# Splitting the second mixer's input projections, and opening the second MLP's accumulators with transposes

## The chip, the core and the metric

The kernel is one program on one core of a Trainium2 chip. Its metric is the device time of one execution in microseconds; the time given for it is the median of three runs. Five engines matter here and run side by side, each through its own instructions in order: TensorE (PE in the profile, with its weight loads as PEld), VectorE (DVE), ScalarE (ACT), GpSimd (POOL), and SyncE (SP), which here only issues the transfers from HBM. All of them wait for one another through semaphores.

## The reference

The input is 256 tokens of 1024 fp32 features. Two layers, each a mixer and an MLP with a residual add behind each, and a norm at the end:

```python
for layer in range(DEPTH):              # 2
    h = rmsnorm(x, mix_norm[layer])
    y = mixer_ab(h, ...) if layer % 2 == 0 else mixer_c(h, ...)
    x = x + y
    x = x + sq_relu_mlp(rmsnorm(x, mlp_norm[layer]), w_up[layer], w_down[layer])
return rmsnorm(x, final_norm)

def mixer_c(h, w_in, conv_w, conv_b, w_r, b_r, w_i, b_i, lam, w_out):
    gate, xr = jnp.split(h @ w_in, 2, axis=-1)               # w_in: 1024 x 2048
    xr = causal_depthwise_conv(xr, conv_w) + conv_b          # width 4
    y = rg_lru(xr, w_r, b_r, w_i, b_i, lam) * jax.nn.gelu(gate)
    return y @ w_out                                         # 1024 x 1024
```

`rg_lru` multiplies xr by two block-diagonal matrices (8 blocks of 128 x 128 each), takes sigmoids, and runs a linear recurrence over the tokens. `sq_relu_mlp` is `square(relu(h @ w_up)) @ w_down` with 4096 hidden features. The weights of the second mixer's input, 8 MB, the two MLPs', 64 MB, and the rest are all read once from HBM.

## The kernel before

**Layout.** x is kept transposed as eight tiles xT[0] to xT[7], each 128 features by 256 tokens. A projection's output chunk (128 features) is the sum of eight products over k; each holds a 128 x 128 block of weights in TensorE and streams the 256 columns of tile k. The two MLPs, their down projections and most of their inputs are split: an fp32 value is a rounded high part and a rest (`split_act` for activations; `weights` for weights, by a rounding copy and a subtraction), both of type fp32r, and a product is the sum of three fp32r products, high with high, high with rest, rest with high. The first mixer, the second mixer's input projections, its gates and its output projection multiply plain fp32 instead, which the profile shows as two records for each product.

**Weights.** A unit is the weights of one output chunk (or of one row chunk in the down and output projections), 512 KB; two units make a piece. `piece` gives each piece its home when the program is built. There are five raw buffers (raw0 to raw4, one piece each) and eight pairs of buffers (wh0/wl0 to wh7/wl7). A piece of MLP weights lands in a raw buffer, and each of its units is split into a pair: `weights` issues, for each half of a unit, a rounding copy (`move`, on VectorE or ScalarE, whichever the planner picks) and a subtraction (VectorE). A piece that is used as plain fp32 is not split: the first five of a sequence of such pieces stay in raw buffers, and each later one lands with its two units in the wh and the wl buffer of one pair. Raw buffers and pairs are each handed out in turn. So before the change the second mixer's xr weights and its gate matrices (`ri`) sit in raw buffers, its gate-branch and output weights in pairs.

**Order.** The whole program is recorded as operations with their dependences, and a planner (`Plan.schedule`) sorts each engine's instructions by list scheduling with costs and latencies written in the file; ten rounds, the shortest forecast is emitted. On TensorE an operation goes when it is ready, by priority, and priorities fall along the written order. The splits' priority is lowered a little (`LIFTS`). Transfers keep the written order among themselves on SP's one queue: a transfer that waits for its buffer holds all those written behind it.

**The second mixer.** At the end of the first MLP `out_cols` finishes the accumulators two chunks at a time, and `residual_chunk` adds them to xT, scales by the norm's gain and squares for the norm. Then come, in written order: xr chunks 0 and 1, the norm's sum (`finish_norm`: a product with ones, a square root, a reciprocal giving rstd), xr chunks 2 to 7 with the gates of finished chunks between them, the gate-branch chunks, and the output projection (`out_rows` for rows 0 to 3, then `out_cols` for 4 to 7). Each xr chunk has a tail on VectorE (times rstd, then the four taps of the conv); the gates' sigmoids, exponentials and roots run on ScalarE, which loads another table whenever the kind of function changes. Projections and gates take the four PSUM banks b in turn; a bank is taken again when its last reader is done.

**The second MLP.** Its down projection is not transposed: five accumulators in PSUM hold tokens by features, so that the output can be written as it is. x has to be added there. Before the change this happens on TensorE: in 16 of the row steps, d = 4 to 19, one of the 8 chunks of one of the two token halves is added by two fp32r products of 128 columns with an identity (`identr`), one for the high part and one for the rest of xT[k].

Of the kernel before, what the change touches and what calls it, by code (L numbers as in the profile page):

```python
# [7 lines left out]
F32R = mybir.dt.float32r  # L8
# [3 lines left out]
P = 128  # L12
S = 256
D = 1024
KD = D // P
# [4 lines left out]
NRAW = 5  # L20
# [306 lines left out]
def hybrid_trunk(ctx, tc, x, mix_norm, mlp_norm, w_up, w_down, ab_w_in, ab_conv_w, ab_ln_g, ab_ln_b,  # L327
# [8 lines left out]
    def tl(name, shape=(P, S), dt=F32):  # L336
        return sb.tile(list(shape), dt, name=name)
# [48 lines left out]
    def copy(out, a):  # L386
        return plan.add("V", [("tensor_copy", (out, a), {})], [out], [a], {"V": vcost(fsize(out), not is_psum(a))})
# [27 lines left out]
    def mms(items, after=()):  # L415

        calls, outs, ins, c = [], [], [], 0.0
        for o, l, r, st, sp in items:
            calls.append(("matmul", (o,), {"lhsT": l, "rhs": r, "start": st, "stop": sp, "skip_group_check": True}))
            outs.append(o)  # L420
            ins += [l, r]
            c += max(fsize(r) / 2400.0, 0.0533) * (1 if l.dtype == F32R else 4) + (0.0135 if l.dtype == F32R else 0.005)
        return plan.add("T", calls, outs[:1], ins, {"T": c}, after=after)

    def transposes(items):
        calls = [("transpose", (o, i, d), {}) for o, i, d in items]
        return plan.add("T", calls, [items[0][0]], [i for _, i, _ in items] + [items[0][2]],
                        {"T": 0.109 * len(items)})

    def dma(out, in_, size):  # L430
        return plan.add("S", [("dma_start", (out, in_), {})], [out], [in_], {"S": 0.0}, size=size)


    ident = tl("ident", (P, P))
    identr = tl("identr", (P, P), F32R)
    ones = tl("ones", (P, P))
    pcol = tl("pcol", (P, P))
    wcol = tl("wcol", (P, P))
# [60 lines left out]

    pieces, units = [], []
    homes, pairs = [], {}
    turn = {"raw": 0, "pair": 0, "whole": 0}

    def piece(kind, ap, whole=True):
        n = len(pieces)
        pieces.append((kind, ap))
        us = [len(units), len(units) + 1]  # L510
        units.extend([(n, 0), (n, 1)])
        turn["whole"] = turn["whole"] + 1 if whole else 0
        if turn["whole"] > NRAW:
            i = turn["pair"] % NSPL
            turn["pair"] += 1
            homes.append((whs[i], wls[i]))
        else:
            raw = raws[turn["raw"] % NRAW]
            turn["raw"] += 1
            homes.append((raw[:, :1024], raw[:, 1024:]))  # L520
        if not whole:
            for u in us:
                pairs[u] = turn["pair"] % NSPL
                turn["pair"] += 1
        return us

    def cols(w, c, whole=True):

        return piece("c", w.rearrange("(k p) c -> p k c", p=P)[:, :, c * P:(c + 2) * P], whole)

    def rows(ap, whole=True):
        return piece("r", ap, whole)

    taken = [0, 0]
    got = {}
# [51 lines left out]
    for us in (((u_gate, 4), (u_val, 0)), ((u_q, 8), (u_k, 12))):  # L587
        for c in (0, 2):
            for u, at in us:
                u += cols(w_in, at + c)  # L590
    u_v = rows(wv[:, 0:4]) + rows(wv[:, 4:8])
    wo = ab_w_out[0].rearrange("(k p) c -> p k c", p=P)
    u_o = {}
    for k in (4, 6, 0, 2):
        u_o[k], u_o[k + 1] = rows(wo[:, k:k + 2])
    LAG, TAIL = 4, 4

    def mlp_units(layer):
        up, dn = [], []
        wd = w_down[layer].rearrange("(f p) c -> p f c", p=P)  # L600
        for f in range(0, NF + LAG, 2):
            if f < NF:
                up += cols(w_up[layer], f, False)
            if f >= LAG:
                dn += rows(wd[:, f - LAG:f - LAG + 2], False)
        return up, dn

    u_up, u_dn, u_xr, u_gt, u_co = {}, {}, [], [], []
    u_up[0], u_dn[0] = mlp_units(0)
    for c in range(0, 8, 2):  # L610
        u_xr += cols(c_w_in[0], 8 + c)
        if c == 2:
            u_r, u_i = piece("ri", None)
    for c in range(0, 8, 2):
        u_gt += cols(c_w_in[0], c)
    wco = c_w_out[0].rearrange("(k p) c -> p k c", p=P)
    for k in range(0, 8, 2):
        u_co += rows(wco[:, k:k + 2])
    u_up[1], u_dn[1] = mlp_units(1)


# [9 lines left out]
    xsrc = x[0].rearrange("(t p) d -> p t d", p=P)  # L631
    R = lambda ap: ap.rearrange("a (b p) -> (a b) p", p=P)
    make_identity(nc, ident)
    copy(identr, ident)
    memset(ones, 1.0, "V")
    memset(eps_t, EPS, "V")
    act(tiny[:, 60:61], eps_t, AF.Sqrt)
# [29 lines left out]
    def par(name, c):  # L667
        i = col0[name] + c
        return pcol[:, i:i + 1]


    def project(dst, u, xs):
        w = weights(u)
        for k in range(KD):
            mms([(dst, w[k], xs[k], k == 0, k == KD - 1)])

    def project_wide(b, u, xs):

# [4 lines left out]
    def split_act(src, scale, tag, bufs, engs="V"):  # L683
        t = rot(tag, bufs, (P, 2 * S), F32R)
        h, lo = t[:, :S], t[:, S:]
        if scale is None:
            move(h, src)
            tt(lo, src, h.bitcast(F32), OP.subtract, engs)
        else:
            move(h, src, scale)  # L690
            stt(lo, src, scale, h.bitcast(F32), OP.mult, OP.subtract)
        return h, lo, t

    def scaled(src, scale):
        t = rot("xg", KD)
        move(t, src, scale)
        return t

    def residual_chunk(k, acc, gname, g0, xs):
        tt(xT[k], acc, xT[k], OP.add)  # L700
        g = par(gname, g0 + k)
        xs[k] = scaled(xT[k], g) if gname == "mix" else split_act(xT[k], g, "x", KD)
        if k in (0, KD - 2):
            act(ssum if k == 0 else sumb, xT[k], AF.Square)
        else:
            sq = rot("nsq", 2)
            act(sq, xT[k], AF.Square)
            if k < KD - 2:
                tt(ssum, ssum, sq, OP.add)
            else:  # L710
                tt(sumb, sumb, sq, OP.add)
# [219 lines left out]
        t = [bank("a") for _ in range(4)]  # L931
        return [t[c // 2][:, (c % 2) * S:(c % 2 + 1) * S] for c in range(KD)]

    def out_mm(acc, c, w, xp, start, stop):
        if not isinstance(w, tuple):
            return mms([(acc, w[c], xp, start, stop)])
        mms([(acc, a[:, c, :], b, start and n == 0, stop and n == 2)
             for n, (a, b) in enumerate(((w[0], xp[0]), (w[0], xp[1]), (w[1], xp[0])))])

    def out_rows(accs, u, xp, first):  # L940
        w = weights(u)
        for c in range(KD):
            out_mm(accs[c], c, w, xp, first and c % 2 == 0, False)

    def out_cols(accs, us, xps, done):
        ws = [weights(u) for u in us]
        for c0 in range(0, KD, 2):
            for c in (c0, c0 + 1):
                for i, (w, xp) in enumerate(zip(ws, xps)):
                    out_mm(accs[c], c, w, xp, False, i == len(us) - 1)  # L950
            done(c0)
            done(c0 + 1)

# [187 lines left out]

    blocks = []

    def down_mm(block, w, hp, first, last):
        t, c0, c1, b = block
        s = slice(t * P, (t + 1) * P)
        wh, wl = (q.rearrange("p a b -> p (a b)")[:, c0:c1] for q in w)
        mms([(b[:, :c1 - c0], p[:, s], q, first and n == 0, last and n == 2)
             for n, (p, q) in enumerate(((hp[0], wh), (hp[1], wh), (hp[0], wl)))])

    xsp = {}

    def down_rows(u, hp, d):
        w = weights(u)
        if d == 0:
            blocks.extend((t, c0, c1, bank("a")) for t, c0, c1 in ((0, 0, 512), (0, 512, D), (1, 0, 512), (1, 512, 768)))
            blocks.append((1, 768, D, banks["b"].pop(bank_at["b"] % 4)))
        for block in blocks:
            down_mm(block, w, hp, d == 0, False)
        if 4 <= d < 20:  # L1160

            k, t = divmod(d - 4, 2)
            if t == 0:
                xsp[k] = split_act(xT[k], None, "r", 2)
            for bt, c0, c1, b in blocks:
                if bt == t and c0 <= k * P < c1:
                    mms([(b[:, k * P - c0:(k + 1) * P - c0], q[:, t * P:(t + 1) * P], identr, False, False)
                         for q in xsp[k][:2]])

    _, us, hs = mlp(1, xs, down_rows)  # L1170
    ws = [weights(u) for u in us]
# [2 lines left out]
    for n, block in enumerate(blocks):  # L1174
        t, c0, c1, b = block
        xg, fc = xg2[t], fcol[:, t]
        for i in range(len(us)):
            down_mm(block, ws[i], hs[i], False, i == len(us) - 1)

        part = fc[:, n % 2 if n < 2 else n - 2:][:, :1]  # L1180
        act(fsq[:, :c1 - c0], b[:, :c1 - c0], AF.Square, accum=part)
        tt(xg[:, c0:c1], b[:, :c1 - c0], gfin[:, c0:c1], OP.mult)
        if c1 < D:
            ts(fc[:, 4:5], part, 1.0 / D, EPS if c0 == 0 else fc[:, 4:5], OP.mult, OP.add)
            continue
        act(fc[:, 5:6], part, AF.Sqrt, scale=1.0 / D, bias=fc[:, 4:5])
        recip(fc[:, 6:7], fc[:, 5:6])
        for h in (slice(0, 512), slice(512, D)):
            move(xg[:, h], xg[:, h], fc[:, 6:7])
            dma(o_dst[:, t, h], xg[:, h], P * 2048)  # L1190
# [32 lines left out]
```

## Time and profile before

| | |
|---|---|
| time, median of 3 runs (lowest to highest) | 589.08 us (588.99 to 589.18) |
| profiled execution: its time, and the span of its instructions | 588.62 us, 586.8 us |
| TensorE busy, mean granted clock | 579.9 us (99%), 0.999 |
| VectorE busy | 413.1 us (70%) |
| ScalarE busy | 289.7 us (49%) |
| read from HBM | 97.11 MB |
| second mixer: input projections and gates | from 307.6 to 370.2 us |
| second mixer: output projection | from 370.2 to 397.9 us |

Busy time is the time in which at least one instruction of the engine runs. TensorE's products overlap one another: the pace of a stream is the time from the start of one to the start of the next, and not the duration of one, which is longer. The same holds for two instructions that follow each other on VectorE or ScalarE. Nearly all instructions are recorded under line 310, the planner's emission, so that groups are told apart by their tiles: x is the scaled and split input of an MLP, xg the scaled plain input of a mixer, f the split hidden activations, raw, wh and wl the weights, r the split xT that the identity products read, arena everything that is small or short-lived. The 1.8 us by which the profiled execution's time exceeds its span lie around the instructions.

### The profile page before, as it was taken

To read this page: it belongs to the slowest core of one execution; us is meant where nothing else is said; L and a number is where in the kernel's file an instruction comes from. 1 tells how busy PE (TensorE), PEld (TensorE's weight loads), DVE (VectorE), ACT (ScalarE), POOL (GpSimd) and SP (SyncE) were. 2 spreads that over 40 slices of the span, in tenths; PEclk is the share of its full clock that TensorE was granted. 3 is DMA by queue.
4 is the path that set the end of the run, shared out by engine and by line. 5 is a ranking of instruction groups with operands and counts; after the bars stand their busy time and mean duration, and the time that the engine had idled before them with its cause. 6 is when DMAs were issued, how large, how long until landed. Compare 5 with 4: busy or idle time off the path is not lost.

```text
span 586.8 us, 9026 instructions
## 1 busy us (share of the span) xinstructions
PE 579.9 (99%) x3305; PEld 510.2 (87%) x3305; DVE 413.1 (70%) x946; ACT 289.7 (49%) x592; POOL 2.8 (0%) x22
## 2 busy tenths in 40 slices
PE   9999999999999999999999999999999999999995
PEld 8888768889999999999998888888888888888885
DVE  2599998599777767677446777559876767767732
ACT  4131435467554555555321798327555555545523
POOL 1000000000000000000000000000000000000000
PEclk9999999999999999999999999999999999999999
DMA  7997704125664665566677005924645664563001
GB/s 222 324 382 256 258 1 144 71 70 163 203 212 145 191 217 166 166 205 203 218 223 280 1 0 157 370 83 143 196 164 180 196 198 144 185 212 107 1 1 72
DMA packets 67612, 98.74 MB, mean 168 GB/s; under 512 B 3212, under 2 KB 55664, under 8 KB 67568
## 3 DMA queue, kind: packets, MB, share of 16 engines
q1 hardware_dynamic: 67568, 98.17, 50.7%
q8 instruction: 26, 0.43, 0.3%
q14 instruction: 18, 0.15, 0.1%
HBM read 97.11 MB, written 1.05 MB: 167 GB/s over the span
## 4 chain that ended last, share of the span: by engine, by line
PE 99%; ACT 0%; DVE 0%; issue 0%; ACTq 0%
PE bank_b L310 56%; PE bank_a L310 42%; ACT arena L395 0%; DVE arena L310 0%; ACT arena L310 0%; DVE ones L310 0%; DVE tiny L310 0%; DVE eps L310 0%; ACTq L310 0%
## 5 line engine op out<-in xcount | busy, mean ns | idle before, releaser
L310 DVE TENSOR_TENSOR wl<-raw,wh 128x512 fp32r<-128x512 f32 x256 | 175.1, 690 | 84.5 <-ACT wh L395 76.3
L395 ACT ACTIVATE wh<-raw 128x512 fp32r<-128x512 f32 x223 | 139.5, 630 | 168.2 <-PE bank_b L310 104.3
L310 PE MATMUL bank_b<-x,wh 128*128 128x512 f32 x512 | 184.7, 401 | 0.0
L310 PE MATMUL bank_b<-x,wl 128*128 128x256 f32 x512 | 143.8, 281 | 0.0
L310 PEld LDWEIGHTS bank_b<-x,wh 128*128 128x128 f32 x512 | 96.4, 188 | 20.9
L310 PEld LDWEIGHTS bank_b<-x,wl 128*128 128x128 f32 x512 | 96.8, 189 | 0.1
L310 PE MATMUL bank_a<-f,wh 128*128 128x256 f32 x512 | 93.2, 283 | 0.0
L310 PEld LDWEIGHTS bank_a<-f,wh 128*128 128x128 f32 x512 | 79.6, 191 | 1.4
L310 PE MATMUL bank_a<-f,wl 128*128 128x256 f32 x256 | 72.4, 283 | 0.0
L310 PE MATMUL bank_a<-wh,f 128*128 128x512 f32 (+1 forms) x256 | 72.2, 364 | 0.0
L310 PE MATMUL bank_b<-xg,raw 128*128 128x256 f32 x288 | 64.1, 379 | 0.0
L310 PEld LDWEIGHTS bank_b<-xg,raw 128*128 128x128 f32 x288 | 54.1, 190 | 7.3
L310 PEld LDWEIGHTS bank_a<-wh,f 128*128 128x128 f32 x256 | 45.9, 188 | 9.1
L310 DVE SCALAR_TENSOR_TENSOR arena<-arena,wcol 128x256 f32<-128x256 f32 x120 | 49.5, 478 | 0.0
L310 PEld LDWEIGHTS bank_a<-f,wl 128*128 128x128 f32 x256 | 49.0, 192 | 0.0
L310 PE MATMUL bank_a<-wl,f 128*128 128x512 f32 (+1 forms) x128 | 46.5, 363 | 0.0
L310 PE MATMUL bank_a<-arena,wh 128*128 128x256 f32 x128 | 34.4, 381 | 0.0
L310 PE MATMUL bank_a<-arena,wl 128*128 128x256 f32 x128 | 33.9, 379 | 0.0
L310 DVE TENSOR_TENSOR relu<-bank_b,relu 128x256 f32<-128x256 f32 x64 | 26.7, 417 | 10.1 <-ACT relu L310 10.1
L310 ACT ACT_TABLE_LOAD x24 | 30.8, 1283 | 3.0 <-PE bank_b L310 1.9
L310 ACT ACTIVATE relu<-relu 128x256 f32<-128x256 f32 x64 | 26.1, 411 | 8.2 <-DVE relu L310 5.1
L310 ACT ACTIVATE relu<-bank_b 128x256 f32<-128x256 f32 x64 | 23.6, 369 | 11.6 <-PE bank_b L310 11.6
(125 smaller groups left out, 594.3 us busy)
## 6 DMA issues: line engine op xcount, KB each, us to landing
raw<-in_w_up_dram SPq DMA_DIRECT2D x64, 512.0 KB, 5.7
raw<-in_w_down_dram SPq DMA_DIRECT2D x64, 512.0 KB, 4.8
raw<-in_c_w_in_dram SPq DMA_DIRECT2D x8, 512.0 KB, 5.4
raw<-in_ab_w_in_dram SPq DMA_DIRECT2D x6, 512.0 KB, 7.8
wh<-in_ab_w_in_dram SPq DMA_DIRECT2D x5, 512.0 KB, 8.7
wl<-in_ab_w_in_dram SPq DMA_DIRECT2D x5, 512.0 KB, 8.8
raw<-in_ab_w_in_dram SPq DMA_DIRECT2D x8, 256.0 KB, 5.7
wh<-in_ab_w_out_dram SPq DMA_DIRECT2D x4, 512.0 KB, 10.0
```

Of the source, the lines that this page charges most:

```text
L310: r.append(getattr(self.engines[o.eng], method)(*map(sub, a), **{n: sub(v) for n, v in k.items()}))
L395: return e.activation(sub(out), sub(a), AF.Copy, **({"scale": scale} if ap else {}))
```

## The change

Two things, independent of each other.

The 16 units of the second mixer's input projection are now split like the MLP's: their pieces land in raw buffers, each unit takes a pair, and a product over k becomes three fp32r products of 256 columns (`mm`, which is the old `out_mm` under a new name with its arguments in another order). `residual_chunk` splits the scaled input of that mixer too. The homes change with it: `piece` is now told its place, "raw", "pair" or "split", by its caller, and the gate matrices `ri` and the output weights take pairs.

The second MLP's accumulators begin with transposes: in step d = 0 the sixteen 128 x 128 blocks of xT are transposed into the five banks by TensorE with the fp32 identity (`flip`), the first block of each bank with the start flag, and all products of the down projection add to that. The 32 products with `identr`, the splits of xT for them, and `identr` are gone.

```diff
+    def flip(out, in_, first):
+        return plan.add("T", [("matmul", (out,), {"lhsT": in_, "rhs": ident, "start": first, "stop": False, "is_transpose": True,
+                                                  "skip_group_check": True})], [out], [in_, ident], {"T": 0.109})
...
-    identr = tl("identr", (P, P), F32R)
...
-    def piece(kind, ap, whole=True):
+    def piece(kind, ap, place):
...
-        turn["whole"] = turn["whole"] + 1 if whole else 0
-        if turn["whole"] > NRAW:
+        if place == "pair":
...
-        if not whole:
+        if place == "split":
             for u in us:
                 pairs[u] = turn["pair"] % NSPL
                 turn["pair"] += 1
...
     for c in range(0, 8, 2):
-        u_xr += cols(c_w_in[0], 8 + c)
+        u_xr += cols(c_w_in[0], 8 + c, "split")
         if c == 2:
-            u_r, u_i = piece("ri", None)
+            u_r, u_i = piece("ri", None, "pair")
     for c in range(0, 8, 2):
-        u_gt += cols(c_w_in[0], c)
+        u_gt += cols(c_w_in[0], c, "split")
     wco = c_w_out[0].rearrange("(k p) c -> p k c", p=P)
     for k in range(0, 8, 2):
-        u_co += rows(wco[:, k:k + 2])
+        u_co += rows(wco[:, k:k + 2], "pair")
...
-    copy(identr, ident)
...
+    def mm(dst, w, k, x, first, last):
+        ps = ((w[0][:, k], x[0]), (w[0][:, k], x[1]), (w[1][:, k], x[0])) if isinstance(w, tuple) else ((w[k], x),)
+        mms([(dst, a, b, first and n == 0, last and n == len(ps) - 1) for n, (a, b) in enumerate(ps)])
+
     def project(dst, u, xs):
         w = weights(u)
         for k in range(KD):
-            mms([(dst, w[k], xs[k], k == 0, k == KD - 1)])
+            mm(dst, w, k, xs[k], k == 0, k == KD - 1)
...
-        g = par(gname, g0 + k)
-        xs[k] = scaled(xT[k], g) if gname == "mix" else split_act(xT[k], g, "x", KD)
+        xs[k] = split_act(xT[k], par(gname, g0 + k), "x", KD)
...
-    def down_mm(block, w, hp, first, last):
+    def down_mm(block, w, hp, last=False):
...
-    xsp = {}
...
             blocks.append((1, 768, D, banks["b"].pop(bank_at["b"] % 4)))
+
+            for t, c0, c1, b in blocks:
+                for k in range(c0 // P, c1 // P):
+                    flip(b[:, k * P - c0:(k + 1) * P - c0], xT[k][:, t * P:(t + 1) * P], k * P == c0)
         for block in blocks:
-            down_mm(block, w, hp, d == 0, False)
-        if 4 <= d < 20:
-
-            k, t = divmod(d - 4, 2)
-            if t == 0:
-                xsp[k] = split_act(xT[k], None, "r", 2)
-            for bt, c0, c1, b in blocks:
-                if bt == t and c0 <= k * P < c1:
-                    mms([(b[:, k * P - c0:(k + 1) * P - c0], q[:, t * P:(t + 1) * P], identr, False, False)
-                         for q in xsp[k][:2]])
+            down_mm(block, w, hp)
```

More of the change, by code (lines that the diff above doesn't have):

```diff
@@ L504, in hybrid_trunk @@
     homes, pairs = [], {}
-    turn = {"raw": 0, "pair": 0, "whole": 0}
-    def piece(kind, ap, whole=True):
+    turn = {"raw": 0, "pair": 0}
+    def piece(kind, ap, place):
         n = len(pieces)
@@ L525, in piece, with cols, rows @@
         return us
[L527 to L532, printed above, removed]
+    def cols(w, c, place):
+        return piece("c", w.rearrange("(k p) c -> p k c", p=P)[:, :, c * P:(c + 2) * P], place)
+    def rows(ap, place):
+        return piece("r", ap, place)
     taken = [0, 0]
@@ L589, in hybrid_trunk @@
             for u, at in us:
-                u += cols(w_in, at + c)
-    u_v = rows(wv[:, 0:4]) + rows(wv[:, 4:8])
+                u += cols(w_in, at + c, "raw" if len(pieces) < NRAW else "pair")
+    u_v = rows(wv[:, 0:4], "pair") + rows(wv[:, 4:8], "pair")
     wo = ab_w_out[0].rearrange("(k p) c -> p k c", p=P)
@@ L594, in hybrid_trunk @@
     for k in (4, 6, 0, 2):
-        u_o[k], u_o[k + 1] = rows(wo[:, k:k + 2])
+        u_o[k], u_o[k + 1] = rows(wo[:, k:k + 2], "pair")
     LAG, TAIL = 4, 4
@@ L602, in mlp_units @@
             if f < NF:
-                up += cols(w_up[layer], f, False)
+                up += cols(w_up[layer], f, "split")
             if f >= LAG:
-                dn += rows(wd[:, f - LAG:f - LAG + 2], False)
+                dn += rows(wd[:, f - LAG:f - LAG + 2], "split")
         return up, dn
@@ L932, in accumulators @@
         return [t[c // 2][:, (c % 2) * S:(c % 2 + 1) * S] for c in range(KD)]
[L934 to L938, printed above, removed]
     def out_rows(accs, u, xp, first):
@@ L942, in out_rows @@
         for c in range(KD):
-            out_mm(accs[c], c, w, xp, first and c % 2 == 0, False)
+            mm(accs[c], w, c, xp, first and c % 2 == 0, False)
     def out_cols(accs, us, xps, done):
@@ L949, in out_cols @@
                 for i, (w, xp) in enumerate(zip(ws, xps)):
-                    out_mm(accs[c], c, w, xp, False, i == len(us) - 1)
+                    mm(accs[c], w, c, xp, False, i == len(us) - 1)
             done(c0)
@@ L1147, in down_mm @@
         wh, wl = (q.rearrange("p a b -> p (a b)")[:, c0:c1] for q in w)
-        mms([(b[:, :c1 - c0], p[:, s], q, first and n == 0, last and n == 2)
+        mms([(b[:, :c1 - c0], p[:, s], q, False, last and n == 2)
              for n, (p, q) in enumerate(((hp[0], wh), (hp[1], wh), (hp[0], wl)))])
-    xsp = {}
     def down_rows(u, hp, d):
@@ L1177, in hybrid_trunk @@
         for i in range(len(us)):
-            down_mm(block, ws[i], hs[i], False, i == len(us) - 1)
+            down_mm(block, ws[i], hs[i], i == len(us) - 1)
         part = fc[:, n % 2 if n < 2 else n - 2:][:, :1]
```

## The prediction

> **What bounds the kernel now.** The page comes first: its busy times, and the shares of the chain of work that ended last.
>
> ```profile
> span 586.8 us, 9026 instructions
> PE 579.9 (99%) x3305; PEld 510.2 (87%) x3305; DVE 413.1 (70%) x946; ACT 289.7 (49%) x592; POOL 2.8 (0%) x22
> ...
> PE 99%; ACT 0%; DVE 0%; issue 0%; ACTq 0%
> ```
>
> A busy TensorE could still be a waiting one, so the waits by engine come second, and the same chain in order of time third. The one wait of PE, and the pieces around the second mixer:
>
> ```profile
> PE bank_a L310 <- DVE eps L310: 1.0, 1, 1.0
> ```
>
> ```profile
> 307.63 62.60 PE bank_b L310 x290
> 370.23 27.68 PE bank_a L310 x128
> ```
>
> PE waits once, at the very start. From 307.63 to 397.9 its products follow one another without a gap (307.63 + 62.60 = 370.23). So this stretch is worth what its products cost, and a product saved is time saved as long as VectorE and ScalarE still deliver in time.
>
> **The split projections, on PE.** The first piece has 290 records: 256 of the 128 plain products (16 units of 8), 32 of the 16 gate products, 2 of the norm's sum; two records each, 145 products, 62.60 / 145 = 0.4317 us. The output projection agrees, 27.68 / 64 = 0.4325. The new form, three fp32r products of 256 columns with weights held and activations streamed, stands in the first MLP's row units, 24 products of that shape each:
>
> ```profile
> 139.16 2.87 PE bank_a L310 x24
> 142.03 2.83 PE bank_b L310 x16
> ```
>
> 2.87 / 24 = 0.1196, three of them 0.359 us. The change takes 128 x (0.4317 - 0.359) = **9.3 us** from PE. Bounds: 0.354 for a k by the MLP's other form (2.83 / 8, a wider product) would give 9.9; 0.120 each gives 9.2.
>
> **The transposes, on PE.** What goes is read from the pace of the second MLP's steps, with identity products and without:
>
> ```profile
> 437.55 2.87 PE bank_b L310 x16
> ...
> 507.55 2.87 PE bank_b L310 x16
> ```
>
> ```profile
> 530.35 3.19 PE bank_b L310 x19
> ...
> 552.72 3.19 PE bank_b L310 x19
> ```
>
> Twelve steps take 70.00 us, 5.833 each; four later ones 22.37, 5.593 each. Two identity products cost 0.24 us, 16 such steps 3.85 us. What comes is 16 transposes of 128 columns. They stand in the trace among other products:
>
> ```profile
> 20.44 0.61 PE L310 MATMUL bank_a<-arena,ones 128*128 128x128 f32 x4
> 20.88 0.38 PE L310 MATMUL bank_a<-ident,arena 128*128 128x128 f32 x2
> 21.10 2.12 PE L310 MATMUL bank_b<-xg,raw 128*128 128x256 f32 x9
> ```
>
> Two transposes take 21.10 - 20.88 = 0.22 us of PE's time, 0.11 each; 16 make 1.76. The upper bound is a plain fp32 product of the same size, two of which (four records) take 20.88 - 20.44 = 0.44: 0.22 each, 3.5 for 16. I take 0.11, the same operation on the same shape: **2.1 us** saved (0.3 at the other bound). They need xT, done since the end of the second mixer, and the five banks, which the down products of that step need anyway, so they wait for nothing new. The eight splits of xT that go (VectorE and ScalarE) lie beside products that never waited for them: nothing. The copy to identr is behind the constants that PE's first product waits for: nothing.
>
> One rule of the Trainium skill speaks against this half. "TensorE: Matmul & The Clock Gate", Part 4: PE-mode transpose, gives about 275 ns for a 128 x 128 transpose in one kernel's context; 16 of them would be an estimated 4.4 us, and this half would lose 0.5. The trace has that number too, as the mean duration of one:
>
> ```profile
> L310 PE MATMUL bank_b<-ident,arena 128*128 128x128 f32 x32 | 5.5, 278 | 0.0
> ```
>
> But at 20.88 the next product began 0.11 us a transpose later: 278 ns is how long one is under way, not how far apart two start. By this trace the rule is no price of a stream.
>
> **What the splits ask of the other engines.** Each of the 16 units now needs four halves' worth of work: two rounding copies and two subtractions; each of the 8 input chunks a second operation on VectorE.
>
> ```profile
> L310 DVE TENSOR_TENSOR wl<-raw,wh 128x512 fp32r<-128x512 f32 x256 | 175.1, 690 | 84.5 <-ACT wh L395 76.3
> L395 ACT ACTIVATE wh<-raw 128x512 fp32r<-128x512 f32 x223 | 139.5, 630 | 168.2 <-PE bank_b L310 104.3
> ...
> L310 DVE SCALAR_TENSOR_TENSOR x<-xT,pcol,x 128x256 fp32r<-128x256 f32 x16 | 7.0, 479 | 0.0
> ```
>
> ```profile
> 370.74 1.29 DVE L310 TENSOR_TENSOR wl<-raw,wh 128x512 fp32r<-128x512 f32 x2 [0.40 <-ACT wh L395]
> ```
>
> Two subtractions take 1.29, so the second adds 1.29 - 0.69 = 0.60 when they follow one another. 32 cost VectorE 19.2 us; 32 copies cost ScalarE up to 20. The cover, by the view of stretches:
>
> ```profile
> 287.50:299.00 11.50, 11.50 (x91) 11.12 (x90) 2.55 (x6) 2.44 (x6) 0.00 (x0) 1.00 0.83 270
> 307.60:375.00 67.40, 67.40 (x314) 59.26 (x313) 47.16 (x111) 45.37 (x76) 0.00 (x0) 1.00 0.40 141
> ```
>
> After the busy times of PE and PEld come VectorE's (47.16) and ScalarE's (45.37). Units 0 to 3 take pairs 1 to 4, whose last readers are row steps of the first MLP before 296; VectorE idles 9.0 us between 287.5 and 299, enough for their eight subtractions (4.8). The other 24 come after 307.6. There the mixer's own work is 47.16 less eight subtractions that belong to the next MLP (4.8), 42.4 us; with 24 x 0.60 and two late input splits it is about 57.6. It has to be done when the output projection's second half begins: 307.6 + (62.6 - 9.3) + 32 x 0.4325 = 374.7, 67.1 us later. VectorE is 86% full. ScalarE, by the same count, has 45.37 less nine of the next MLP's copies (5.6) plus 24 x 0.63, 54.9 of 67.1, 82%. Tight, but covered; a split is needed only unit by unit, and the planner gives them slack. If that cover were gone, every us over 67.1 would be a us on the path.
>
> **The queue.** SP issues in written order, and `ri` is written between xr weights 0 to 3 and 4 to 7. Its home was a raw buffer; now it is pair 5, which the first unit of the first MLP's closing `out_cols` holds almost to the end. Before, all xr weights were on their way by 286; a transfer to a pair of that closing was let go at 306.46:
>
> ```profile
> 277.42 8.99 SPq L310 DMA_DIRECT2D raw<-in_c_w_in_dram  x4
> ...
> 306.46 0.34 SPq L310 DMA_DIRECT2D wh<-in_c_w_out_dram  x1
> ```
>
> So now xr units 4 to 7 and the whole gate branch queue behind `ri` until about 306.5. Rates, while `ri` was moving before and for full rows:
>
> ```profile
> 276.00:277.00 1.00, 1.00 (x10) 1.00 (x10) 0.30 (x1) 0.90 (x2) 0.00 (x0) 1.00 1.02 288
> 309.00:310.00 1.00, 1.00 (x6) 0.90 (x5) 0.68 (x2) 0.25 (x1) 0.00 (x0) 1.00 1.00 401
> ```
>
> `ri`, 1.05 MB at 288 GB/s, takes 3.6 us, half a piece of xr 1.8. Bytes start about 1 us after the issue: unit 4's first half is in at about 313, the second at 315; copy and subtraction (0.63 + 0.69 and hand-overs) make it ready at 314.5 and 316.5. PE comes to unit 4 after four units and the norm's sum: 307.63 + 4 x 2.87 + 0.43 = 319.5. Three us of slack where there were thirty.
>
> A second place that gets close: xr chunk 3 takes the bank of chunk 0, which VectorE frees once rstd is there.
>
> ```profile
> 313.51 0.59 PE L310 MATMUL bank_b<-ssum,ones 128*128 128x256 f32 x2
> ```
>
> ```profile
> 314.65 1.75 DVE L310 RECIPROCAL rstd<-rstd 128x256 f32<-128x256 f32 x1 [4.49 <-ACT rstd L310]
> 316.51 0.76 DVE L310 TENSOR_TENSOR arena<-bank_b,rstd 128x256 f32<-128x256 f32 x2
> ```
>
> The bank is free 3.4 us after the sum starts (313.51 to 316.9). With two units in front, the sum would start at 313.4 and PE be ready for chunk 3 at 307.63 + 3 x 2.87 + 0.43 = 316.7: a stall of 0 to 0.3 us, none if the planner pulls the sum ahead by some products, as it did before. I allow **0.4 us** for these two places and the gates' banks (bounds 0 and 3).
>
> **The sum**, against the profiled execution's own time: 588.62 - 9.3 - 2.1 + 0.4 = 577.6. That execution lies 0.46 under the median of the runs, so for the median 578.1; I say **578.0**.
>
> **Rivals.**
>
> *The weights come late.* If `ri`, in its short rows, moves at half the rate, it takes 7.2 us and unit 4 is ready at about 318 to 320, units 5 to 7 hard behind it; and ScalarE and VectorE, in order, hold rstd and the xr tails behind a split that waits for data. Against it: 288 GB/s in the row above, and PE's written order has other products only from the gates on, which need those tails. Price 3 to 5 us: about **582**. Chance 0.15.
>
> *The transposes cost more.* At 0.22 each, as plain products: 1.8 us more, about **579.8**. The page's 275 ns would give an estimated 580.7. For it: these write into banks that later products add to, which no transpose of the trace does. Chance 0.09.
>
> *The splits become the path* (the other side). A unit's split takes about 2.0 us from free pair to ready (a copy 0.63, two subtractions, hand-overs), against 2.87 on PE. If units could be split only when PE is done with the unit before, each of the 12 not split early would add 2.0 us: 578 + 24 = 602. It decides from six units on (11.4 saved / 2.0). Against it: with eight pairs a unit waits for one used seven or eight units earlier, except gate-branch unit 3, whose pair `ri` holds until the last gate, one unit ahead of it. For it: ScalarE's table loads, 15 in that stretch, which stand in front of its copies:
>
> ```profile
> L310 ACT ACT_TABLE_LOAD x15 | 19.2, 1283 | 0.3
> ```
>
> Chance 0.05.
>
> **How the numbers follow.** The forecast has 0.71. Its own range, from no stall with the cheaper products (577.1) to 1.5 us of stalls (579.3), reaches through the transposes' rival and most of the late weights': 576.8 to 582.5 leaves out the far end of the late weights and the splits as path. Differences under 0.2% (1.2 us) are no change that this measurement can tell. All cases but the last are faster by more; of the last I give 0.03 to slower, and 0.02 to a partly exposed split that ends within 0.2%: faster 0.95, same 0.02, slower 0.03.
>
> **What would show it.** Right: the second mixer's projections and gates in 53.3 us instead of 62.6 without a wait of PE; 24 records of fp32r to a unit at 0.12 each; steps of the second MLP at 5.59 us throughout, the first longer by 1.8; VectorE near 85% from 307 to 375. Wrong: PE waiting for wl or for a bank between 313 and 345, `ri` landing after 312, a transposes' stretch of 3.5 us, or a lower granted clock behind a stall.

## The result, and the profile after

| | before | after |
|---|---|---|
| time, median (lowest to highest) | 589.05 us (588.99 to 589.18) | 578.15 us (577.69 to 579.17) |
| profiled execution: time, span | 588.62, 586.8 us | 578.12, 576.3 us |
| second mixer: projections and gates | 62.6 us | 54.0 us |
| second mixer: output projection | 27.7 us | 27.7 us |
| second MLP up to its last four row units | 171.95 us | 169.84 us |

The ratio of the times is 0.9817, 95% interval 0.98 to 0.9834: 10.9 us less, and 0.15 us from the predicted 578.0, a tenth of the 1.5 us by which the four runs after spread.

The page after, in the lines that answer to those of before:

```profile
span 576.3 us, 9336 instructions
PE 569.4 (99%) x3417; PEld 507.2 (88%) x3417; DVE 430.8 (75%) x978; ACT 300.9 (52%) x613; POOL 2.7 (0%) x22
...
PE 92%; ACT 4%; DMA 3%; issue 1%; DVE 0%; SPq 0%; ACTq 0%
```

TensorE is still the engine that is always busy, but the chain no longer runs through it alone: ScalarE and the transfers have 7% of it, 40 us. The same chain in order of time shows where (start, duration, what; the longest pieces):

```profile
293.53 14.41 PE bank_a L310 x120
308.90 6.24 DMA raw<-in_c_w_in_dram
315.62 8.84 DMA raw<-in_c_w_in_dram
347.56 14.42 PE bank_b L310 x118
361.98 27.68 PE bank_a L310 x128
389.67 14.31 PE bank_b L310 x82
...
559.51 9.62 PE bank_a L310 x48
```

and, of the chain before, the ends of the second MLP's stretch up to its last four row units:

```profile
397.91 14.31 PE bank_b L310 x82
...
569.86 9.62 PE bank_a L310 x48
```

From 308.9 to 347.6 the chain goes through the second mixer's weights and ScalarE, although TensorE hardly stops: a chain follows what came last, by however little. The ends of the pieces give the account. The second mixer starts at 293.53 + 14.41 = 307.94, 0.31 later than before; it takes 54.04 us instead of 62.60; the output projection is unchanged; from 389.67 to the last four row units at 559.51 the second MLP takes 169.84 instead of 569.86 - 397.91 = 171.95, 2.11 less; the end is 0.15 shorter. 0.31 - 8.56 - 2.11 - 0.15 = -10.5, the difference of the spans.

The transposes, in TensorE's timeline:

```profile
403.81 1.69 PE L310 MATMUL bank_a<-ident,xT 128*128 128x128 f32 x14
405.34 0.38 PE L310 MATMUL bank_b<-ident,xT 128*128 128x128 f32 x2
405.48 0.71 PE L310 MATMUL bank_a<-wh,f 128*128 128x512 f32 x2
```

Sixteen in 405.48 - 403.81 = 1.67 us, 0.104 each.

The stalls of the second mixer, in the same timeline (in brackets what ended an idle time), and the waits of the weight loads:

```profile
339.71 0.59 PE L310 MATMUL bank_b<-arena,wl 128*128 128x256 f32 x2
340.29 0.51 PE L310 MATMUL bank_b<-x,wh 128*128 128x256 f32 x2
...
347.00 0.40 PE L310 MATMUL bank_b<-x,wh 128*128 128x256 f32 x2
347.56 0.39 PE L310 MATMUL bank_b<-x,wl 128*128 128x256 f32 x1 [0.15 <-DVE wl L310]
```

```profile
PEld bank_b L310 <- ACT arena L310: 0.4, 1, 0.4
...
PEld bank_b L310 <- DVE wl L310: 0.4, 1, 0.4
```

Two groups of two records take 0.58 and 0.56 us to the next start where such groups take 0.25 otherwise: 0.65 us of stalls in all, one before a bank that ScalarE had to read, one before a subtraction.

The load of the other engines, by stretches (after PE and PEld come VectorE and ScalarE):

```profile
307.76:374.70 66.94, 66.79 (x480) 63.77 (x479) 61.98 (x142) 55.23 (x98) 0.00 (x0) 1.00 0.75 246
320.50:362.00 41.50, 41.35 (x316) 39.96 (x315) 40.33 (x96) 40.09 (x70) 0.00 (x0) 1.00 0.59 195
```

Between 320.5 and 362 VectorE and ScalarE are both 97% busy, and TensorE is at 99.6% (41.35 of 41.50).

### The profile page after: what moved, and what is told of

The parts are those of the page before. It is cut to its first block, busy times and chain, and to the rows that moved or that the text cites. A ratio compares the mean times of both kernels' runs of the same rounds, so it can differ in the third digit from the quotient of the medians.

```text
span 576.3 us, 9336 instructions
## 1 busy us (share of the span) xinstructions
PE 569.4 (99%) x3417; PEld 507.2 (88%) x3417; DVE 430.8 (75%) x978; ACT 300.9 (52%) x613; POOL 2.7 (0%) x22
## 3 DMA queue, kind: packets, MB, share of 16 engines
HBM read 97.11 MB, written 1.05 MB: 170 GB/s over the span
## 4 chain that ended last, share of the span: by engine, by line
PE 92%; ACT 4%; DMA 3%; issue 1%; DVE 0%; SPq 0%; ACTq 0%
PE bank_b L310 49%; PE bank_a L310 43%; DMA raw<-in_c_w_in_dram 3%; ACT arena L310 1%; ACT L310 1%; ACT wh L395 1%; SPq L310 0%; ACT arena L395 0%; DVE wl L310 0%; DVE arena L310 0%; DVE ones L310 0%; DVE tiny L310 0%; ACTq L395 0%; DVE wh L396 0%; DVE eps L310 0%
## 5 line engine op out<-in xcount | busy, mean ns | idle before, releaser
L310 DVE TENSOR_TENSOR wl<-raw,wh 128x512 fp32r<-128x512 f32 x288 | 196.4, 690 | 81.6 <-ACT wh L395 78.1
L395 ACT ACTIVATE wh<-raw 128x512 fp32r<-128x512 f32 x252 | 156.6, 630 | 167.9 <-PE bank_b L310 106.6
L310 PE MATMUL bank_b<-x,wh 128*128 128x512 f32 (+1 forms) x768 | 231.3, 362 | 0.0
L310 PE MATMUL bank_b<-x,wl 128*128 128x256 f32 x640 | 180.4, 282 | 0.2 <-DVE wl L310 0.2
L310 PEld LDWEIGHTS bank_b<-x,wh 128*128 128x128 f32 x768 | 136.8, 190 | 21.2 <-ACT arena L310 0.4
L310 PEld LDWEIGHTS bank_b<-x,wl 128*128 128x128 f32 x640 | 121.6, 190 | 0.5 <-DVE wl L310 0.4
L310 PE MATMUL bank_b<-xg,raw 128*128 128x256 f32 x160 | 36.1, 382 | 0.0
L310 PEld LDWEIGHTS bank_b<-xg,raw 128*128 128x128 f32 x160 | 30.2, 192 | 4.0
L310 DVE SCALAR_TENSOR_TENSOR relu<-relu,rstd 128x256 f32<-128x256 f32 x64 | 26.8, 424 | 1.8
```

What stands on the lines that cost most here:

```text
L310: r.append(getattr(self.engines[o.eng], method)(*map(sub, a), **{n: sub(v) for n, v in k.items()}))
L395: return e.activation(sub(out), sub(a), AF.Copy, **({"scale": scale} if ap else {}))
```

## The experiments

The theory: TensorE's products set the time in both halves, and the halves add up. The rivals: the halves are no sum; a transpose costs as much as a plain product; and for the small rest of stalls, either the queue (weights late behind the gate matrices), or ScalarE's table loads, or VectorE's load.

**Each half alone.** `e1_split_only` is the changed kernel with the identity products back:

```diff
-            for t, c0, c1, b in blocks:
-                for k in range(c0 // P, c1 // P):
-                    flip(b[:, k * P - c0:(k + 1) * P - c0], xT[k][:, t * P:(t + 1) * P], k * P == c0)
...
+                    mms([(b[:, k * P - c0:(k + 1) * P - c0], q[:, t * P:(t + 1) * P], identr, False, False)
+                         for q in xsp[k][:2]])
```

> The split projections alone; x is added by the 32 identity products as before. If TensorE's products set the end, this is before less what the second mixer's stretch lost in the changed kernel's trace (62.6 to 54.2 us, 8.4): 580.6, and the steps of the second MLP are back at 5.83 us. Rival, the two halves are no sum (what the one gives, the other has given already, or the planner's new order gives part of it): more than 1 us away from 580.6.

Measured: 580.03 us, 0.9849 of before (0.9834 to 0.9864), 9.0 less. The chain:

```profile
308.09 53.64 PE bank_b L310 x418
361.73 27.69 PE bank_a L310 x128
```

That is 0.6 under the expected sum, inside its 1 us. The second mixer takes 53.64 us here, one unbroken piece, 0.4 less than in the changed kernel's trace; the changed kernel itself took 53.51 in another execution (`e12`, below), so the 0.4 can't be put down to the edit. The second MLP up to its last four row units takes 561.36 - 389.42 = 171.94 us again.

`e2_flip_only` is before with the transposes in place of the identity products and nothing else.

> The transposes alone; the second mixer as before. Transposes at the pace of 0.11 us: 16 take 1.76 us, 32 identity products go (3.85 us), 587.0. At the pace of plain products (0.22): 588.7. At 275 ns each: 589.6, slower than before.

Measured: 587.04 us, 0.9966 (0.9954 to 0.9979), 1.99 less; the second MLP's stretch takes 567.91 - 398.06 = 169.85 us, 2.10 less. 9.0 + 1.99 = 11.0 against 10.9 for both: the halves add up, and neither the price of a plain product (588.7) nor 275 ns a transpose (589.6) fits.

**The price of a transpose by itself.** `e4_plain_product`:

```diff
-    "stop": False, "is_transpose": True,
+    "stop": False,
```

> The 16 transposes run as plain fp32 products of the same blocks with the same identity, which rounds x differently and changes nothing else. If a transpose costs half a plain product (0.11 against 0.22): 1.75 us more than the changed kernel, 579.9, and their stretch 3.5 us instead of 1.7. If the pace of such small products is set by loading the held block, the same for both: 578.1.

Measured: 580.40 us, 0.9856 (0.9842 to 0.9869), 2.25 more than the changed kernel. TensorE's timeline:

```profile
404.60 3.29 PE L310 MATMUL bank_a<-ident,xT 128*128 128x128 f32 x28
407.72 0.61 PE L310 MATMUL bank_b<-ident,xT 128*128 128x128 f32 x4
408.08 0.71 PE L310 MATMUL bank_a<-wh,f 128*128 128x512 f32 x2
```

Two records for each block now, and 408.08 - 404.60 = 3.48 us, 0.2175 a block: twice the transpose, 1.81 us more in all. The rival of one pace for both, 578.1, falls. The profiled execution is 2.6 us longer than that of the changed kernel; the rest of these lies in the second mixer (54.65 us against 54.04) and ahead of it (0.2).

**The queue.** `e3_gates_behind` writes `ri` behind all xr weights:

```diff
-        if c == 2:
+        if c == 6:
             u_r, u_i = piece("ri", None, "pair")
```

> The gate matrices are written behind all xr weights, so that xr weights 4 to 7 no longer queue behind a transfer that waits for its pair. If the queue makes the second mixer's remaining 0.9 us of stalls: ScalarE's waits for the mixer's weights (5.3 us after the change) go, the stretch takes 53.3 instead of 54.2 us, 577.3. Rival, the stalls (at 340 and 347 us) come from ScalarE, full with table loads, and VectorE behind it: 578.1, as the changed kernel, with the waits for weights gone all the same.

Measured: 578.14 us, 0.9817 (0.9803 to 0.983): nothing. But it did not do what it was meant to. The xr weights went early, all let go by 284, but ScalarE's waits for the mixer's weights did not go:

```profile
ACT wh L395 <- DMA raw<-in_c_w_in_dram: 6.2, 4, 5.1
...
PEld bank_b L310 <- ACT arena L310: 1.0, 1, 1.0
```

Now the gate branch's weights queue behind `ri`, whose pair comes free only after xr chunk 0, and TensorE's one stall, 0.9 us at 343.5, is before a bank that ScalarE still has to read. This run tells nothing apart.

`e8_gates_raw` puts `ri` into a raw buffer, as before the change; `e9_gates_raw_behind` does so and writes it behind all xr weights, so that the buffer it takes is needed by nobody until the next MLP:

```diff
-        if c == 2:
-            u_r, u_i = piece("ri", None, "pair")
+        if c == 6:
+            u_r, u_i = piece("ri", None, "raw")
```

> The gate matrices go to a raw buffer, as before the change: nothing waits for a pair any more, all xr weights are early, but the buffer is free only after the last gate (344 us), and the last four gate-branch units queue for it: in at about 349, split at 351, for a use at 350.5. If the queue is what matters: 0.5 to 1.5 us more than the changed kernel, 578.6 to 579.6. If ScalarE's tables make the stalls: 578.1, about as the changed kernel.

> The gate matrices are written behind all xr weights and go to a raw buffer that nothing needs before the next MLP: no weights of the second mixer wait for a pair, a last gate or one another. If late weights, which push ScalarE's copies and VectorE's subtractions into the stretch of the gates, make the 0.9 us of stalls: the stretch takes 53.3 to 53.4 us without a wait of TensorE, 577.2. If ScalarE's table loads make them by themselves: 54.2 us as in the changed kernel, 578.1.

Measured: `e8` 577.87 us, 0.9806 (0.9792 to 0.9821); `e9` 577.88, 0.9808 (0.9794 to 0.9821). The chain of `e9` through the second mixer, and that of `e8`:

```profile
308.20 53.39 PE bank_b L310 x418
361.59 27.69 PE bank_a L310 x128
```

```profile
306.90 53.39 PE bank_b L310 x418
360.29 27.69 PE bank_a L310 x128
```

Both are without a stall, at about the 53.3 us worked out for the products alone, and `e8` with more table loads on ScalarE (17 between 300 and 375) than the changed kernel had (13): so 17 table loads alone made no stall here. What is left is the late weights, which push copies and subtractions into the stretch where both engines are full. This is argued and not shown: in the profiled executions the stretch took 53.39 us in three kernels with early weights (`e8`, `e9`, and `e11` below) and 53.51 to 54.65 with the weights as late as in the changed kernel (two of that kernel, `e1`, `e4`), but `e10`, with early weights and more splits, stalls too. In `e8` the last gate-branch weights, let go at 342.6, came in time, against the expectation. In the time, though, neither can be told from the changed kernel; that was run once more beside `e9`.

> The changed kernel itself once more, beside the three others on the same chip, since they differ from it by less than 1%: 578.1, with the spread of its first runs (577.7 to 579.2).

Measured: 578.13 us, 0.9818 (0.9804 to 0.9832), from 577.68 to 579.31. Its profile:

```profile
307.94 53.51 PE bank_b L310 x418
361.45 27.68 PE bank_a L310 x128
```

The same program with the same late weights, and in this execution no stall to speak of: 53.51 instead of 54.04 us. So the stalls of the changed kernel are not in every execution. The longest times (579.2, 579.3) are above all of those of `e9` (577.36 to 578.11), which fits stalls of about 1 us in some executions, but this is argued from few runs.

`e7_gates_twice` goes the other way:

```diff
-                dma(home.rearrange("p (k c) -> p k c", k=KD), ...)
+                for _ in range(2):
+                    dma(home.rearrange("p (k c) -> p k c", k=KD), ...)
```

> The gate matrices are loaded twice, one after the other, so that everything behind them on the queue is 4 to 6 us later. After the change unit 4 was split at 317.6 and 320.1 us for a use at 319.3 and 320.8: if that slack is gone, TensorE waits for it, 3 to 5 us more: 581 to 583. If the planner or the queue has slack left: 578 to 579.

Measured: 581.20 us, 0.9868 (0.9853 to 0.9883), 3.05 more than the changed kernel. The waits of PE and PEld:

```profile
PE bank_b L310 <- ACT arena L310: 1.3, 1, 1.3
...
PE bank_b L310 <- ACT wh L395: 1.0, 1, 1.0
PE bank_b L310 <- DVE wl L310: 0.5, 2, 0.3
```

But it delayed more than was meant. Each second load waited until the first had landed, as SP's waits show:

```profile
SPq L310 <- DMA wl<-in_c_w_i_dram: 4.8, 1, 4.8
SPq L310 <- DMA wh<-in_c_w_r_dram: 4.6, 1, 4.6
```

The first xr transfer behind `ri` was let go at 316.95 instead of 308.90, 8 us later and not 4 to 6, and unit 4's first copy began at 322.19 instead of 315.16, 7 us later. Of these 7 us some 3 came through, a part at unit 4 (from 321 to 326), a part at a gates' bank that ScalarE still had to read (1.3 us at 346 to 348). The planner had put the gates of two chunks (319.66 to 322.87) in front of unit 4. So weights that come much later are paid for, but not us for us.

**VectorE's cover.** `e5_sub_twice_gt` and `e6_sub_twice_all`, with `u_gt` or `u_xr + u_gt` in the condition:

```diff
-                tt(wl[:, q], half[h], wh[:, q].bitcast(F32), OP.subtract)
+                for _ in range(2 if v in u_gt else 1):
+                    tt(wl[:, q], half[h], wh[:, q].bitcast(F32), OP.subtract)
```

> The 16 subtractions of the gate-branch units are made twice (same result): 9.6 us more on VectorE, which after the change is busy 62.0 of the 66.9 us between 307.8 and 374.7, and 40.3 of 41.5 from 320.5 to 362. If a full engine there means that it sets the pace: 5 to 9 us more than the changed kernel, 583 to 587. If VectorE's work has slack where it counts (10 subtractions of the next MLP, 6 us, and the recurrence can go later, since the output projection takes rows one by one): 0 to 3 us more, 578 to 581.

> All 32 subtractions of the second mixer's units twice: 19.2 us more on VectorE, 4.8 of it before 307. Work of the mixer alone then is 57.6 + 14.4 = 72.0 us for 67: at least 5 us more than the changed kernel, 583, if only the sum counts; 9 us and more, above 587, if the xr tails come late too. Nothing more (578) if VectorE were no limit at all.

Measured: 580.29 us (0.9851, 0.9836 to 0.9866), 2.1 more than the changed kernel for 9.6 us of work; 582.81 us (0.9893, 0.9877 to 0.991), 4.7 more for 19.2. The stretches of the first and of the second:

```profile
307.70:374.70 67.00, 65.50 (x473) 62.29 (x472) 62.98 (x141) 48.74 (x86) 0.00 (x0) 1.00 0.65 214
```

```profile
307.70:374.70 67.00, 63.98 (x464) 60.56 (x463) 64.86 (x141) 47.79 (x86) 0.00 (x0) 1.00 0.57 190
```

VectorE is hardly busier (62.98, 64.86 against 61.98): the work of the next MLP moves out of the stretch. In the changed kernel 34 subtractions of weights lie there, 24 of the mixer and 10 of the next MLP; in `e5` 40 (24 and the 16 added), in `e6` 48 (24 twice), so by these counts none of the next MLP. The first is within the expectation of slack, the second 0.2 us under the 583 of "if only the sum counts". An engine that is 97% busy had slack, because what it did was not all due; about a quarter of what is added comes through. Whether that quarter comes from the sum of the work or from single units that are ready later is not told apart here.

**A further step: the output projection split too.** On top of `e9`:

```diff
-        u_co += rows(wco[:, k:k + 2], "pair")
+        u_co += rows(wco[:, k:k + 2], "split")
...
-        mx[c] = gi[c]
+        mx[c] = split_act(gi[c], None, "f", LAG + 3) if c < KD - 1 else split_act(gi[c], None, "m", 1)
```

`e11_output_half` does it for rows 4 to 7 alone.

> As the run before, and the second mixer's output projection is split too: 64 products at 0.359 instead of 0.4325 us, 4.7 us less on TensorE; 16 subtractions (9.6 us), 16 copies and 8 more splits of its input (2.7 us on VectorE) come in the stretch where VectorE is busiest. If they fit (10 subtractions of the next MLP, 6 us, give way): 572.5. If VectorE is the limit there, 12.3 us more of work less 6 that can go later are lost again: about as the run before, 577 to 579.

> As the run before, with only rows 4 to 7 of the output projection split (the half that comes last): 2.35 us less on TensorE, 8 subtractions and 4 splits of input, 6.1 us more on VectorE. If they fit: 574.9. If VectorE is the limit: 577 or more.

Measured: `e10` 574.30 us, 0.975 (0.9736 to 0.9764); `e11` 575.80 us, 0.9776 (0.9762 to 0.979). The chain of `e10`, and that of `e11`:

```profile
346.39 16.46 PE bank_b L310 x135
362.85 23.04 PE bank_a L310 x192
385.89 14.57 PE bank_b L310 x82
```

```profile
307.62 53.39 PE bank_b L310 x418
361.01 25.33 PE bank_a L310 x160
386.35 14.56 PE bank_b L310 x82
```

The projection falls from 27.69 to 23.04 us, by 4.65, and to 25.33 by half of it, as the products say. Against `e9` (577.88) the times are 3.6 and 2.1 us less, where a full fit would have been 4.7 and 2.35: both lie nearer to "they fit" than to VectorE as the limit. `e10` loses about 0.5 us again before one gate bank, and the next MLP's first piece takes 14.57 instead of 14.31. It is the fastest kernel of this study, 14.7 us below before.

## Why the prediction was right

*The split projections, 9.3 us.* Right to a tenth: without a stall the stretch takes 53.39 us (`e8`, `e9`), 62.60 - 53.39 = 9.2. In the changed kernel's own profile it is 8.56, less by the stalls.

*The transposes, 2.1 us.* Right: 2.11 in the profile, 1.99 in `e2`. 0.104 us each instead of 0.11, and the product behind them is longer by 0.08 (0.54 us to the next start instead of 0.46), 1.75 us in all against 1.76; the bound by plain products, 0.22, was what `e4` measured for those (0.2175). The rival with dearer transposes falls. The 275 ns that the Trainium skill gives ("TensorE: Matmul & The Clock Gate", Part 4: PE-mode transpose) fall as a price too: by them `e2` would have taken an estimated 589.6 us, and it took 587.04.

*The cover.* For VectorE 57.6 us of the mixer's own work were worked out; 61.98 were busy, with 10 subtractions of the next MLP among 34, some 6 us: 56. For ScalarE 54.9, and 55.23 were busy, of which copies of the next MLP are a part. The size was right; the view was too wide. Over 67 us the engines are 93% and 82% busy, but between 320.5 and 362 both are at 97%, and that is where the stalls are. That a part of the work can be moved out, `e5` and `e6` show.

*The queue, three us of slack.* The term that was mis-sized. Unit 4 was to be ready at 316.5. In the timelines of ScalarE and VectorE after:

```profile
315.16 0.63 ACT L395 ACTIVATE wh<-raw 128x512 fp32r<-128x512 f32 x1 [2.70 <-DMA raw<-in_c_w_in_dram]
```

```profile
317.60 0.69 DVE L310 TENSOR_TENSOR wl<-raw,wh 128x512 fp32r<-128x512 f32 x1
...
319.39 0.69 DVE L310 TENSOR_TENSOR wl<-raw,wh 128x512 fp32r<-128x512 f32 x1
```

Its first half came at 315.1, not 313, and its subtractions stood behind xr tails on VectorE until 317.6 and 319.4: ready at 320.1, for a use at about 321. One us of slack, not three. `ri` was let go when the prediction said (306.75 against 306.5), but it and the half piece behind it, 1.57 MB, were in only after about 7 us (308 to 315), some 225 GB/s, although the queue moved 282 GB/s in these 7 us: the transfers written behind moved their bytes at the same time, which a sum of sizes over one rate leaves out. The rival of late weights had unit 4 ready at 318 to 320, and so it came; but its price of 3 to 5 us did not follow, since unit 4's halves (318.3 and 320.1) were still ahead of their uses. That price came only with 7 us more of delay (`e7`).

*The 0.4 us of stalls.* 0.65 in the first profile, 0.1 in that of the second run of the same kernel. Neither of the two places named first was it: the norm's sum was pulled ahead (at 311.4) and freed the bank in time, and unit 4 came just in time. It was the third, the gates' banks behind ScalarE, and a subtraction. Two of the prediction's signs of being wrong came true in a small size: PE waited for a bank at 340, and `ri` was in at 312 at the earliest, since the bytes of all transfers from 306 to 312 add up to 1.06 MB and `ri` is 1.05.

*The sum.* For the profiled execution 577.6 was worked out, and it took 578.12: 0.25 more of stalls, 0.1 less saved by the projections, 0.31 of a later start that no term stood for, and an end 0.15 shorter. That the medians meet within 0.15 us is luck; the terms are each right to some tenths of a microsecond.

*The splits as path.* Nothing of it: units were split ahead of their use, and even 32 subtractions more kept the kernel 6.2 us below before.

## What to carry to other kernels

Where one engine's products follow one another without a gap, a count of products times their pace, read from start to start in the same trace, gives a change's worth to a few tenths of a microsecond; the mean duration of one instruction does not. What has then to be shown is that the engines that pay for it deliver in time, and for that the busy share is read over the narrow stretch in which their work is due, with the question which of it could go later. A buffer that is handed out in another order moves waits into the transfer queue, where everything written behind inherits them. Here that was worth no measurable time: with `ri` written elsewhere (`e3`, `e8`, `e9`) the kernel took 577.87 to 578.14 us, the changed kernel 578.13.

## What the runs showed of the hardware

A transpose of a 128 x 128 fp32 block takes TensorE 0.104 us in a row of sixteen, and a plain fp32 product of the same blocks 0.2175 us, in two records (`e4`). Two fp32r products with 128 columns cost a step of before 0.24 us, as much as two with 256 (2.87 / 24 each). In the timeline they take only 0.17 us to the next start (443.06 to 443.23), but the wide product behind them takes 0.29 instead of 0.24: what they cost lies in part on the product behind them, and the 32 identity products were dearer than their columns suggest. Not expected either: the first 13 us, in which the first weights arrive and which no edit is meant to touch, differ by up to 1.7 us from one profiled execution to another (the first long run of the first mixer's products starts at 12.20 us in that of `e8`, 12.83 before, 13.22 after, 13.92 in that of `e10`), nearly as much as the second half of this change is worth.
